# Transposed block inverses in a buffer of their own, and made first

## The chip, the cores and the metric

The kernel runs on one core of one Trainium2 chip. The metric is the device time of one execution in microseconds (us). The engines are TensorE (PE; its weight loads are shown apart as PEld), VectorE (DVE), ScalarE (ACT), GpSimd (POOL) and SyncE (SP), which issues nearly all DMAs. Each engine works through its own instructions in the order in which they stand in the program.

## The reference

One inference step of a two-layer trunk over 128 context and 512 latent tokens (640 in all, width 1024). Each layer runs three mixers side by side: grouped attention (A), latent attention (B), and a recurrent mixer (C) with 8 heads of 64 channels, run over the tokens forwards and backwards. The change lies in mixer C, whose recurrence per head is

```
sa    = einsum('bhij,bhj->bhi', state, a_t)
state = state * w_t + sa ⊗ b_t + v_t ⊗ k_t
y_t   = einsum('bhij,bhj->bhi', state, r_t)
```

The kernel does this in chunks of 64 tokens: inside a chunk the terms `sa` of all tokens solve a unit triangular system, so it needs the inverse of one 64x64 triangular matrix for each head, direction and chunk.

## The kernel before

**Tiling and stages.** Activations lie channel-major, 128 channels to a tile, 640 tokens along the free dimension. A layer has a phase of input projections and mixer C, then attention, then merge and output projection. Mixer C takes the heads in four pairs `p` = 0 to 3; with two layers that makes eight rounds, called here the first to the eighth. A round has these steps:

- `c_inproj` and `c_prep`: projections of key and receptance, decays, the operands `L1` and `BK` (DVE lines 546 to 553);
- `c_pairs`: 40 products on PE into `pA` (line 612), masked into `L1` and `AB` (lines 615, 617, 620 to 625), and transposes of `BK` (lines 632 to 636);
- `c_inverse`: the inverse of the 40 triangular matrices, in place in `AB`; the change lies here;
- `c_scan`: the recurrence over the chunks, with short PE products that wait for ACT and DVE in turn (lines 771 to 803);
- `c_gn` and `c_out` (lines 818 to 852): group normalisation and output.

**The inverse.** A 64x64 matrix is taken as 2x2 blocks of 32x32. Lines 653 and 655 copy the two diagonal blocks of all matrices into `NF`, line 656 transposes them, so that one partition of `LN` holds a whole 32x32 block. Thirty steps of substitution follow on DVE (lines 662 and 664), each needing the one before. Then line 666 transposes the inverses back into `NF`, lines 671 (ACT) and 673 (DVE) copy them into the diagonal of `AB`, and line 674 writes into the same `NF` the inverses once more, this time transposed within each block. PE takes those as moving operand of the first product `px` (line 683, 32x32 matmuls); its result goes to `X1`, which lies in `LN` (lines 688 DVE, 690 ACT), and enters the second product `py` (line 695), whose result becomes the off-diagonal block of `AB` (lines 700, 702). `py` also reads the copies of lines 671 and 673; `px` does not: it reads `NF` and the off-diagonal block of `AB`.

**What sets the order.** The program is written as generators: while the scan of round `p` is written, `pump` writes pieces of the next round's projections, pairs and inverse and of independent projections, called fillers here (the matmuls of lines 227 to 229 and their weight preparation on ACT line 176 and DVE line 177). The table `PLAN` says how many fillers go to each round. The context manager `TileContext(..., schedule_with_timeline_sim=True)` then sets the order of instructions on each engine when the program is built, so a change in one place can move instructions in others. The buffers `NF` and `LN` exist once and serve all rounds.

Of the kernel before, what the change touches and what calls it, by code (L numbers as in the profile page):

```python
# [10 lines left out]
F32 = mybir.dt.float32  # L11
# [82 lines left out]
def f32(ap):  # L94
    return ap.bitcast(F32)
# [12 lines left out]
class Trunk:  # L108
# [230 lines left out]
    def c_open(self, ctx, ctx2, l):  # L339
        tc, nc, I = self.tc, self.nc, self.I  # L340

        def pool(ctx, name, bufs, **k):
            return ctx.enter_context(tc.tile_pool(name=f"{name}{l}", bufs=bufs, reuse_waits="tile", **k))


        self.ct = pool(ctx, "ct", 5)
        self.ce = ce = pool(ctx, "ce", 1)
        cpe = pool(ctx, "cpe", 1)

        self.cs = pool(ctx2, "cs", 1, side="right")  # L350
        self.cp = [cpe, pool(ctx2, "cpo", 1, side="right")]
        self.cmask = ce.tile([128, T], mybir.dt.bfloat16, tag="cmask", name="cmask")
        self.G.memset(self.cmask, 1.0)
        self.G.memset(self.cmask[:, ::64], 0.0)
        self.amask = ce.tile([128, 2, 128], F32, tag="amask", name="amask")
        nc.sync.dma_start(out=self.amask, in_=I["amask"])
        self.NF = ce.tile([128, 1024], F32, tag="NF", name="NF")
        self.LN = ce.tile([128, 1024], F32, tag="LN", name="LN")
        self.G.memset(self.NF, 0.0)

        self.wul = ce.tile([128, 2, 128], F32R, tag="wul", name="wul")
        self.wua = ce.tile([128, 2, 128], F32, tag="wua", name="wua")

        self.wbd = [self.cs.tile([128, 2, 2, 64], F32, tag=f"wbd{i}", name=f"wbd{i}") for i in range(2)]
        self.ubd = [self.cs.tile([128, 2, 2, 64], F32, tag=f"ubd{i}", name=f"ubd{i}") for i in range(2)]
        for t_ in (self.wul, self.wua, *self.wbd, *self.ubd):
            self.G.memset(t_ if t_ is not self.wul else f32(t_), 0.0)
# [270 lines left out]
    def c_inverse(self, e, ps):  # L638

        V, S, G, PE = self.V, self.S, self.G, self.PE  # L640
        AB = e.AB

        def pc(name):
            return ps.tile([128, 512], F32, tag="g", name=name)


        NF, LN = self.NF, self.LN
        NFv = NF.rearrange("p (t u) -> p u t", u=32)
        for q in range(4):
            rows = slice(32 * q, 32 * q + 32)  # L650
            cs_ = slice(32 * (q % 2), 32 * (q % 2) + 32)
            if q % 2:
                S.copy(out=NFv[rows, 0:20, :], in_=AB[rows, :, 0, cs_])
            else:
                V.tensor_copy(out=NFv[rows, 0:20, :], in_=AB[rows, :, 0, cs_])
        V.transpose(out=LN, in_=NF)
        LNv = LN.rearrange("p (a b) -> p a b", b=32)
        prt = NF
        for s in range(1, 31):
            m = 31 - s  # L660
            pv_ = prt[:, 0:m * s].rearrange("p (a b) -> p a b", b=s)
            V.tensor_tensor(out=pv_, in0=LNv[:, s + 1:32, s:s + 1].to_broadcast([128, m, s]),
                            in1=LNv[:, s:s + 1, 0:s].to_broadcast([128, m, s]), op=ALU.mult)
            V.tensor_tensor(out=LNv[:, s + 1:32, 0:s], in0=LNv[:, s + 1:32, 0:s], in1=pv_, op=ALU.add)
        G.memset(LN[:, 0:1024:33], 1.0)
        V.transpose(out=NF, in_=LN)
        for q in range(4):
            rows = slice(32 * q, 32 * q + 32)
            cs_ = slice(32 * (q % 2), 32 * (q % 2) + 32)
            if q % 2 == 0:  # L670
                S.copy(out=AB[rows, :, 0, cs_], in_=NFv[rows, 0:20, :])
            else:
                V.tensor_copy(out=AB[rows, :, 0, cs_], in_=NFv[rows, 0:20, :])
        V.transpose(out=NF, in_=LN.rearrange("p (a b) -> p b a", b=32))

        A0 = (slice(0, 32), slice(64, 96))
        A1 = (slice(32, 64), slice(96, 128))
        X1 = LN[:, 0:T].rearrange("p (u x) -> p u x", x=32)
        for u0, n in ((0, 10), (10, 10)):
            px = pc("px")  # L680
            for h in range(2):
                for j in range(n):
                    PE.matmul(px[A1[h], j * 32:j * 32 + 32], lhsT=AB[A0[h], u0 + j, 0, 32:64],
                              rhs=NFv[A0[h], u0 + j, :], start=True, stop=True)
            for h in range(2):
                src = px[A1[h], 0:n * 32].rearrange("p (u x) -> p u x", x=32)
                if u0 == 0:
                    V.tensor_copy(out=X1[A1[h], u0:u0 + n], in_=src)
                else:
                    S.copy(out=X1[A1[h], u0:u0 + n], in_=src)  # L690
        for u0, n in ((0, 10), (10, 10)):
            py = pc("py")
            for h in range(2):
                for j in range(n):
                    PE.matmul(py[A0[h], j * 32:j * 32 + 32], lhsT=X1[A1[h], u0 + j, :],
                              rhs=AB[A1[h], u0 + j, 0, 32:64], start=True, stop=True)
            for h in range(2):
                src = py[A0[h], 0:n * 32].rearrange("p (u x) -> p u x", x=32)
                if u0 == 0:
                    V.tensor_copy(out=AB[A0[h], u0:u0 + n, 0, 32:64], in_=src)  # L700
                else:
                    S.copy(out=AB[A0[h], u0:u0 + n, 0, 32:64], in_=src)
# [939 lines left out]
```

## Time and profile before

| | us |
|---|---|
| median of 3 runs | 2241.67 |
| lowest and highest | 2239.26 to 2246.77 |
| the profiled execution: its time | 2248.71 |
| its span, first to last instruction | 2246.9 |
| mean granted TensorE clock, share of 2.4 GHz | 0.954 |

The profiled execution is 7.0 us above the median, and 1.8 us of it lie outside the span. The page of the profile gives busy time and share of each engine, the timeline the single instructions with the idle time of the engine just before them in brackets and what ended it; the windows give the granted clock of a stretch.

### The profile page before, as it was taken

Reading aid. Unit: us, or ns where it says so; the run is one execution under the profiler, and the core shown is the slowest. Engines: PE = TensorE matmul, PEld = TensorE weight load, DVE = VectorE, ACT = ScalarE, POOL = GpSimd, SP = SyncE. Lnnn points to the kernel's source line nnn. Section 1 sums busy time; section 2 is a strip of 40 time slices with the busy share of each in tenths; the row PEclk is TensorE's granted clock in tenths of the full one; section 3 lists DMA queues with packets and bytes.
Section 4 is the critical chain, followed back from the end, with each engine's and each line's share of the span. In section 5 each row is a group of like instructions: output and inputs, shape, how many; then the busy total and the mean of one; then the engine's idle time right before and its main releaser. Section 6 shows DMA issues by size and latency. Waiting matters only on the chain.

```text
span 2246.9 us, 40407 instructions
## 1 busy us (share of the span) xinstructions
PE 2095.5 (93%) x15380; PEld 1993.5 (89%) x15380; DVE 1519.9 (68%) x2998; ACT 1200.9 (53%) x2734; POOL 448.1 (20%) x618
## 2 busy tenths in 40 slices
PE   8999999999789889999989999999998888899998
PEld 6989999999779768889989999999997777788998
DVE  4676887857645677766647767668575567776673
ACT  4544656556353667762345455555453546776332
POOL 3111223213121221102030012222221231111112
PEclk9998999999799899999999999899896999999999
DMA  6232222232223211036612222222222221111552
GB/s 235 79 96 73 91 81 98 92 101 86 88 83 127 84 39 40 32 103 207 198 54 86 96 76 90 64 91 90 81 91 67 94 85 42 34 48 60 183 186 84
DMA packets 111762, 209.70 MB, mean 93 GB/s; under 512 B 14416, under 2 KB 33488, under 8 KB 111568
## 3 DMA queue, kind: packets, MB, share of 16 engines
q1 hardware_dynamic: 111568, 207.12, 28.5%
q8 instruction: 121, 1.98, 0.4%
q14 instruction: 73, 0.60, 0.1%
HBM read 163.52 MB, written 43.55 MB: 92 GB/s over the span
## 4 chain that ended last, share of the span: by engine, by line
PE 73%; DVE 11%; ACT 8%; issue 3%; DMA 3%; POOL 1%; SPq 0%; DVEq 0%; ACTq 0%; POOLq 0%
PE pcm L227 11%; PE pcm L228 11%; PE pcm L229 11%; PE pA L612 3%; PE sc L958 3%; PE sca L771 3%; PE pm L180 2%; PE pm L182 2%; PE pm L181 2%; PE pp L976 2%; PE scb L786 2%; PE scb L777 2%; PE sca L790 2%; PE pout L180 1%; PE pout L182 1%
## 5 line engine op out<-in xcount | busy, mean ns | idle before, releaser
L227 PE MATMUL pcm<-hh,whi 128*128 128x320 f32 x1952 | 628.0, 322 | 19.6 <-ACT xlo L380 4.6
L229 PE MATMUL pcm<-hh,wlo 128*128 128x320 f32 x1952 | 618.2, 317 | 3.5 <-DVE wlo L177 3.5
L228 PE MATMUL pcm<-hl,whi 128*128 128x320 f32 x1952 | 618.6, 317 | 0.0
L227 PEld LDWEIGHTS pcm<-hh,whi 128*128 128x128 f32 x1952 | 374.9, 192 | 27.6 <-ACT xlo L380 5.1
L229 PEld LDWEIGHTS pcm<-hh,wlo 128*128 128x128 f32 x1952 | 374.1, 192 | 5.4 <-DVE wlo L177 4.2
L228 PEld LDWEIGHTS pcm<-hl,whi 128*128 128x128 f32 x1952 | 374.8, 192 | 1.3
L176 ACT CAST whi<-wraw 128x512 fp32r<-128x512 f32 (+1 forms) x356 | 226.1, 666 | 274.8 <-PE pcm L228 109.7
L177 DVE TENSOR_TENSOR wlo<-wraw,whi 128x512 fp32r<-128x512 f32 (+1 forms) x324 | 248.6, 785 | 119.1 <-ACT whi L176 113.8
L782 POOL COPY ubd<-VZ 64x128 f32<-64x128 f32 x160 | 63.3, 395 | 457.0 <-ACT VZ L779 450.5
L961 DVE TENSOR_REDUCE nm<-sc 128x1 f32<-128x640 f32 x128 | 104.3, 819 | 26.9 <-PE sc L958 25.5
L166 DVE TENSOR_TENSOR pl<-pp,ph 128x512 fp32r<-128x512 f32 x160 | 107.1, 684 | 22.2 <-ACT ph L165 19.4
L182 PE MATMUL pm<-yh,wlo 128*128 128x320 f32 x384 | 118.9, 310 | 0.3 <-DVE wlo L177 0.3
L180 PE MATMUL pm<-yh,whi 128*128 128x320 f32 x384 | 118.8, 309 | 0.0
L181 PE MATMUL pm<-yl,whi 128*128 128x320 f32 x384 | 118.7, 309 | 0.0
L963 ACT ACTIVATE P<-sc,nm 128x640 f32<-128x640 f32 x128 | 102.1, 799 | 25.7 <-DVE nm L961 20.8
L165 ACT CAST ph<-pp 128x512 fp32r<-128x512 f32 x160 | 91.8, 588 | 37.9 <-PE pp L976 20.4
L976 PE MATMUL pp<-small,P 128*128 128x128 f32 x640 | 98.2, 278 | 2.7 <-ACT RB L1004 2.2
L771 PE MATMUL sca<-VZ,L 128*128 128x64 f32 x640 | 91.5, 284 | 1.7 <-DVE VZ L803 1.7
L771 PEld LDWEIGHTS sca<-VZ,L 128*128 128x128 f32 x640 | 89.1, 207 | 3.1 <-DVE VZ L803 2.8
L803 DVE SCALAR_TENSOR_TENSOR VZ<-scb,gm,Zg 64x64 f32<-64x64 f32 x256 | 62.2, 280 | 40.6 <-PE scb L786 33.6
L976 PEld LDWEIGHTS pp<-small,P 128*128 128x128 f32 x640 | 78.0, 143 | 12.8 <-ACT RB L1004 4.3
L612 PE MATMUL pA<-L,BK 128*128 128x128 f32 x640 | 85.5, 276 | 4.0 <-ACT AB L617 3.7
(376 smaller groups left out, 4748.7 us busy)
## 6 DMA issues: line engine op xcount, KB each, us to landing
wraw<-in_win SPq DMA_DIRECT2D x156, 256.0 KB, 3.0
wraw<-in_wg SPq DMA_DIRECT2D x96, 256.0 KB, 3.0
wraw<-in_wmod SPq DMA_DIRECT2D x64, 256.0 KB, 3.0
gsp<-gt SPq DMA_DIRECT2D x48, 320.0 KB, 3.3
gt<-gsp SPq DMA_DIRECT2D x48, 320.0 KB, 3.4
wraw<-in_wo SPq DMA_DIRECT2D x24, 512.0 KB, 4.2
cm<-gsl SPq DMA_DIRECT2D x26, 320.0 KB, 3.4
wraw<-in_wmod SPq DMA_DIRECT2D x16, 512.0 KB, 6.5
```

The lines of the kernel that those rows point to most:

```text
L166: self.V.tensor_tensor(out=lo, in0=src, in1=f32(hi), op=ALU.subtract)
L176: self.S.copy(out=hi[part], in_=raw)
L177: sub.tensor_tensor(out=lo[part], in0=raw, in1=f32(hi[part]), op=ALU.subtract)
L180: self.PE.matmul(out, lhsT=lh, rhs=rh, start=first, stop=False)
L181: self.PE.matmul(out, lhsT=lh, rhs=rl, start=False, stop=False)
L182: self.PE.matmul(out, lhsT=ll, rhs=rh, start=False, stop=last)
L227: PE.matmul(p[0:m, 0:H], lhsT=wh[:, kt], rhs=self.hh[:, kt, rs], start=(kt == 0), stop=False)
L228: PE.matmul(p[0:m, 0:H], lhsT=wh[:, kt], rhs=self.hl[:, kt, rs], start=False, stop=False)
L229: PE.matmul(p[0:m, 0:H], lhsT=wl[:, kt], rhs=self.hh[:, kt, rs], start=False, stop=(kt == KT - 1))
L612: PE.matmul(pA[:, j * 128:(j + 1) * 128], lhsT=BK[:, u].rearrange("p a s -> p (a s)"), rhs=L1[h][:, u].rearrange("p a s -> p (a s)"), star ...
L771: PE.matmul(a4[:, d, h], lhsT=L1[h][:, uu[d]].rearrange("p a s -> p (a s)"), rhs=VZ[h][:, cc[d], :], start=(h == 0 and d == 0), stop=False ...
L976: PE.transpose(p[:, qt * 128:(qt + 1) * 128], Ps[qt][:, t * 128:(t + 1) * 128], self.ident)
```

## The change

The transposed inverses get a buffer `NT` of their own. Their transposition moves from behind the copies of lines 671 and 673 to the place right behind the substitution, ahead of the plain transposition of line 666; `px` reads `NT` instead of `NF`. The same instructions are executed, as many as before. Lines behind the edit have higher numbers in the changed program: line 666 becomes 671, 671 and 673 become 676 and 678, 674 becomes 670, 683 becomes 687, and from 675 on a line moves by 4; the lines from 359 to 665 move by 1.

```diff
+        self.NT = ce.tile([128, 1024], F32, tag="NT", name="NT")
...
         G.memset(LN[:, 0:1024:33], 1.0)
+
+        NT = self.NT
+        NTv = NT.rearrange("p (t u) -> p u t", u=32)
+        V.transpose(out=NT, in_=LN.rearrange("p (a b) -> p b a", b=32))
         V.transpose(out=NF, in_=LN)
         for q in range(4):
...
                 V.tensor_copy(out=AB[rows, :, 0, cs_], in_=NFv[rows, 0:20, :])
-        V.transpose(out=NF, in_=LN.rearrange("p (a b) -> p b a", b=32))
...
                     PE.matmul(px[A1[h], j * 32:j * 32 + 32], lhsT=AB[A0[h], u0 + j, 0, 32:64],
-                              rhs=NFv[A0[h], u0 + j, :], start=True, stop=True)
+                              rhs=NTv[A0[h], u0 + j, :], start=True, stop=True)
```

The scheduler answers with a new order from the first inverse on: on PE the first 1055 and the last 2348 of 13350 matmuls stand as before, and in between many have moved. Three places matter below, all in the fourth round (layer 0, `p` = 3).

On DVE, the end of the substitution and what follows it, before:

```order
L662 TENSOR_TENSOR NF<-LN 128x30
L664 TENSOR_TENSOR LN<-LN,NF 128x30
L666 STREAM_TRANSPOSE NF<-LN 128x1024
L673 COPY AB<-NF 32x20x32 x2
L674 STREAM_TRANSPOSE NF<-LN 128x1024
L688 COPY LN<-px 32x320 x2
L700 COPY AB<-py 32x10x32 x2
```

On DVE, the same place now (`L` is the operand `L1` of the round before, written by its group normalisation; `wlo` is a filler's weight):

```order
L663 TENSOR_TENSOR NF<-LN 128x30
L665 TENSOR_TENSOR LN<-LN,NF 128x30
L834 TENSOR_TENSOR BK<-BK,gsb 128x640
L177 TENSOR_TENSOR wlo<-wraw,whi 128x512
L670 STREAM_TRANSPOSE NT<-LN 128x1024
L671 STREAM_TRANSPOSE NF<-LN 128x1024
L837 TENSOR_TENSOR L_3528<-BK,lnx 128x10x64
L177 TENSOR_TENSOR wlo<-wraw,whi 128x512
L678 COPY AB<-NF 32x20x32 x2
L692 COPY LN<-px 32x320 x2
L177 TENSOR_TENSOR wlo<-wraw,whi 128x512
L704 COPY AB<-py 32x10x32 x2
```

The transposition that feeds `px` has moved ahead of the other one and of the copies; four instructions of other work have come in around it.

On PE, around the last pair products `pA` of this round, before:

```order
L612 MATMUL pA<-L_4990,BK 128x128 x4
L771 MATMUL sca<-VZ,L_3527 128x64
L771 MATMUL sca<-VZ,L_3528 128x64 x2
L227 MATMUL pcm<-hh,whi 128x320
L228 MATMUL pcm<-hl,whi 128x320
L229 MATMUL pcm<-hh,wlo 128x320
L227 MATMUL pcm<-hh,whi 128x320
L228 MATMUL pcm<-hl,whi 128x320
L229 MATMUL pcm<-hh,wlo 128x320
L227 MATMUL pcm<-hh,whi 128x320
L228 MATMUL pcm<-hl,whi 128x320
L229 MATMUL pcm<-hh,wlo 128x320
```

On PE, the same place now:

```order
L613 MATMUL pA<-L_4991,BK 128x128 x4
L775 MATMUL sca<-VZ,L_3528 128x64 x2
L775 MATMUL sca<-VZ,L_3529 128x64 x2
L227 MATMUL pcm<-hh,whi 128x320
L228 MATMUL pcm<-hl,whi 128x320
L613 MATMUL pA<-L_4991,BK 128x128 x2
L229 MATMUL pcm<-hh,wlo 128x320
```

The last two products of the round stood behind nine fillers and now stand behind two; counted over the whole order, the last one is number 3268 of PE's matmuls instead of 3326, and 214 fillers lie between it and the first `px` instead of 156.

On PE, around `px` of this round, before:

```order
L899 MATMUL pqt<-small,qcm 128x128 x5
L683 MATMUL px<-NF,AB 32x32 x40
L695 MATMUL py<-AB,LN 32x32 x40
L571 MATMUL pbn<-prh,bones 128x320
L572 MATMUL pbn<-prl,bones 128x320
```

On PE, the same place now:

```order
L903 MATMUL pqt<-small,qcm 128x128 x2
L687 MATMUL px<-NT,AB 32x32 x40
L903 MATMUL pqt<-small,qcm 128x128 x3
L699 MATMUL py<-AB,LN 32x32 x40
L572 MATMUL pbn<-prh,bones 128x320
```

Three transposes of attention (line 899 of before) have moved between the two products; the first `px` is number 3572 instead of 3575.

## Rows read from the trace of the kernel before

**Rows 1.** The page, part 1: busy us, share of span, count by engine.
```profile
PE 2095.5 (93%) x15380; PEld 1993.5 (89%) x15380; DVE 1519.9 (68%) x2998; ACT 1200.9 (53%) x2734; POOL 448.1 (20%) x618
```

**Rows 2.** Waits of PE: who <- for what: us in total, times, longest.
```profile
PE px L683 <- DVE NF L674: 14.7, 3, 12.7
```

**Rows 3.** Timeline of DVE, fourth inverse: start, us, line, operation, [idle before <-releaser].
```profile
591.78 1.25 DVE L666 STREAM_TRANSPOSE NF<-LN 128x1024 f32<-128x1024 f32 x1
593.06 1.40 DVE L673 COPY AB<-NF 32x640 f32<-32x640 f32 x2
595.63 1.91 DVE L674 STREAM_TRANSPOSE NF<-LN 128x1024 f32<-128x1024 f32 x1 [1.17 <-ACT AB L671]
599.88 0.99 DVE L688 COPY LN<-px 32x320 f32<-32x320 f32 x2 [2.34 <-PE px L683]
```

**Rows 4.** Timeline of PE, the same inverse.
```profile
597.59 3.93 PE L683 MATMUL px<-NF,AB 32*32 32x32 f32 x77 [12.66 <-DVE NF L674]
601.30 0.26 PE L695 MATMUL py<-AB,LN 32*32 32x32 f32 x1
```

**Rows 5.** Timeline of all engines, its last pair product and its chain’s start.
```profile
547.03 0.60 PE L612 MATMUL pA<-L,BK 128*128 128x128 f32 x4
...
551.58 1.25 DVE L656 STREAM_TRANSPOSE LN<-NF 128x1024 f32<-128x1024 f32 x1 [0.88 <-ACT NF L653]
```

**Rows 6.** Waits of DVE from 533 to 552 us, ahead of that chain.
```profile
DVE L L615 <- PE pA L612: 5.7, 5, 2.9
```

**Rows 7.** Timeline of all engines, its first pair product.
```profile
513.37 0.91 DVE L548 TENSOR_TENSOR BK<-kd,TM 128x640 f32<-128x640 f32 x1
...
516.91 0.49 PE L612 MATMUL pA<-L,BK 128*128 128x128 f32 x3
```

**Rows 8.** Line 674: duration ns min/median/max, first and last start.
```profile
L674 DVE STREAM_TRANSPOSE NF<-LN x8: 1901/2038/2105, 194.3 to 1700.8; 128x1024 f32<-128x1024 f32 x8
```

**Rows 9.** Line 833, the same columns.
```profile
L833 DVE TENSOR_TENSOR L<-BK,lnx x8: 785/822/825, 339.5 to 1804.1; 128x640 f32<-128x640 f32 x8
```

**Rows 10.** The page, part 5, line 177: busy, mean ns, idle before.
```profile
L177 DVE TENSOR_TENSOR wlo<-wraw,whi 128x512 fp32r<-128x512 f32 (+1 forms) x324 | 248.6, 785 | 119.1 <-ACT whi L176 113.8
```

**Rows 11.** Timeline of PE, filler matmuls three apart, at 190 us.
```profile
190.10 0.31 PE L227 MATMUL pcm<-hh,whi 128*128 128x320 f32 x1
...
190.54 0.31 PE L227 MATMUL pcm<-hh,whi 128*128 128x320 f32 x1
```

**Rows 12.** Timeline of PE, filler matmuls three apart, at 1444 us.
```profile
1444.39 0.47 PE L227 MATMUL pcm<-hh,whi 128*128 128x320 f32 x1
...
1445.19 0.47 PE L227 MATMUL pcm<-hh,whi 128*128 128x320 f32 x1
```

**Rows 13.** Timeline of all engines, seventh inverse.
```profile
1563.34 1.24 DVE L666 STREAM_TRANSPOSE NF<-LN 128x1024 f32<-128x1024 f32 x1
...
1570.06 0.33 PE L683 MATMUL px<-NF,AB 32*32 32x32 f32 x3 [1.64 <-DVE NF L674]
```

**Rows 14.** Timeline of all engines, eighth inverse.
```profile
1695.06 1.25 DVE L666 STREAM_TRANSPOSE NF<-LN 128x1024 f32<-128x1024 f32 x1
...
1702.77 0.36 PE L683 MATMUL px<-NF,AB 32*32 32x32 f32 x3 [4.09 <-DVE mean L823]
```

**Rows 15.** Windows at half clock: us, PE busy (count), granted clock, DMA share, GB/s.
```profile
201.70:211.90 10.20, 10.20 (x88) 0.50 0.30 98
321.20:328.00 6.80, 6.80 (x74) 0.50 0.08 22
457.70:464.50 6.80, 6.80 (x49) 0.50 0.22 66
587.40:618.10 30.70, 19.04 (x208) 0.50 0.12 38
1300.80:1304.20 3.40, 3.40 (x15) 0.50 0.61 187
1427.10:1447.60 20.50, 19.81 (x161) 0.50 0.16 50
```

## The prediction

> **What bounds the kernel now.** I read the page first: PE is busy for 93% of the span [rows 1], so the kernel gains where PE stops waiting, and hardly where only DVE or ACT work less. Next the table of waits on PE. The product `px` waits for line 674 three times, 14.7 us in all, 12.7 of them in one wait [rows 2]; no other wait in that table is as long. The timelines then show where: the fourth inverse (12.66 us, [rows 4]), the seventh (1.64 us, [rows 13]) and the eighth (4.09 us, booked apart in [rows 14], where the row names a short instruction behind line 674; the transposition is what `px` reads). The rest of the 14.7 us is 0.4 us at the second. At the first, third, fifth and sixth inverse fillers stand ahead of `px` and PE does not wait. So the most that the change can remove directly is 14.7 + 4.1 = 18.8 us, 0.8% of the span.
>
> **What the edit itself does.** Nothing is added or removed: eight transpositions to `NT` in place of eight to `NF`, 2.04 us each [rows 8], no DMA, no new semaphore path between other engines. What is shortened is the way from the end of the substitution to `px`. In the fourth inverse it ran over line 666 (1.25 us), the copies on DVE (1.40) and on ACT, a wait of 1.17 for these, and line 674 (1.91): from 591.78 to the start of `px` at 597.59, 5.8 us [rows 3, 4]. Now it is one transposition of 2.04 us: 3.8 us less. In the seventh it was 6.7 us, in the eighth 7.7 us [rows 13, 14], so 4.7 and 5.7 us less.
>
> The second product does not gain as much. The copies of `px` into `X1` are queued on DVE behind everything that was moved back. In the fourth inverse that is, after `NT`: the plain transposition 1.25, line 833 with 0.82 [rows 9], a filler's line 177 with 0.79 [rows 10], two copies 1.40, and the copies of `px` themselves 0.99 [rows 3]: 5.25 us. `px` takes 3.7 us until `py` starts behind it [rows 4]. So PE, which now starts `px` 3.8 us sooner, idles up to 1.5 us between the products (some of it covered by three transposes that now stand there), and 2.2 us are left of the 3.8. This is the price of the new order, and it hits where no filler stands between the products: the fourth, seventh and eighth. In the seventh only the transposition, two copies and the copies of `px` are in the way, 3.6 us, as long as `px`: nothing lost.
>
> **What the scheduler does with it.** The order shows the larger effect. In the fourth round the last pair product stands 58 matmuls earlier on PE, with 214 fillers instead of 156 between it and `px`, while `px` itself is at the same place in PE's sequence. A filler takes 0.147 us at full clock (0.44 for three, [rows 11]), so 58 are 8.5 us: the substitution can start that much sooner while PE has work for that much longer. Does it start sooner? Before, the last pair product started at 547.03 and the chain at 551.58 [rows 5], and in the 19 us ahead of it DVE waited 5.7 us for just these products [rows 6], so DVE has the room. If the whole 8.5 us come through, the substitution ends at 591.78 − 8.5 = 583.3, `NT` is ready at 585.3, PE arrives at 597.59 − 12.66 = 584.9 and waits 0.4; `py` starts 5.25 us after `NT`, at 590.6 instead of 601.30: 10.7 us gained. If only the 5.7 us come through, 7.9 us. Against it stands a possible new wait: the first pair product of the round is 9.8 us earlier on PE; before, it started 2.6 us after its last operand from DVE was ready (513.37 + 0.91 to 516.91, [rows 7]), and in DVE's order the operands are about 3 us earlier. 9.8 − 2.6 − 3.0 = 4.2 us is the most it can wait, and none if DVE, which waits for PE in this stretch too, moves up as well. Bounds for the fourth inverse: 2.2 us (the chain starts no sooner) to 10.7; I take 8.5, near the middle of 7.9 and 10.7 less a small new wait.
>
> Eighth: four passes of the group normalisation over 640 columns (lines 818 to 828) now stand ahead of the transposition, 4 × 0.82 = 3.3 us. `NT` is ready at 1695.06 + 3.3 + 2.04 = 1700.4, `px` gains 2.4 of its 4.09 us, and `py`, behind 5.3 us of DVE work instead of 3.7 of `px`, gains 0.8. Bounds 0 to 4.1; I take 1.0. Second: its 0.4 us go, since fillers now stand ahead of `px`. Seventh: here the scheduler works against it. The last pair product is 37 matmuls later on PE (5.3 us) and two more normalisation passes (1.6 us) lie inside the chain, while `px` is at the same place. `NT` is ready between 1563.34 + 1.6 + 2.0 = 1567.0 and 5.3 us later, 1572.3, against a start of 1570.06: between 1.6 gained (PE arrives only at 1568.42) and 2.2 lost; I take 0.3 lost. At the other four, `px` has moved forward by 5 to 44 fillers (0.7 to 6.5 us) and what it reads is ready 3.8 us or more sooner; I cost them at nothing, covered by the fillers still ahead of `px`; without that cover each would cost up to the 2.7 us by which the third outruns its 3.8.
>
> **The clock.** After the 32x32 products the granted clock falls to half (1.2 of 2.4 GHz): six such stretches are shown, 3.4 to 30.7 us long [rows 15]. A filler then takes 0.267 instead of 0.147 us [rows 12], so 45% of such a stretch is lost where PE has work. The two shortest before, 6.8 and 3.4 us at the third and fifth inverse, are those with 22 fillers between `px` and `py`. The first and sixth get that form now: from 10.2 and 20.5 to about 5 each, 20.7 us × 0.45 = 9.3 us gained. The second, which had none between, now gets a scan step and six fillers there, the form of the sixth before with 20.5 us: 13.7 us more, 6.2 lost. Net 3.1 gained; since the stretches come in few, coarse lengths I take 1.4, bounds −6 to +9.
>
> **Sum.** 8.5 + 1.0 + 0.4 − 0.3 + 1.4 = 11.0 us. Against the profiled execution's own time: 2248.7 − 11.0 = 2237.7. That execution is 7.0 us above the median of the three runs; I take the difference as the same in an execution at the median, so 2241.7 − 11.0 = 2230.7, say 2231 us. Its own range, from the ends of the fourth inverse and half the clock's bounds: 2224 to 2236.
>
> **Rivals.**
>
> *The wait moves to DVE.* The substitution is bound by DVE's own queue and starts no sooner in the fourth round; then only the shorter way counts: 2.2 + 0.8 + 0.4 − 2.2 = 1.2 us, with the clock's 1.4 about 2.6: 2239, no change that can be told. For it: in the chain itself DVE hardly idles, and PE's order alone does not speed it. Against it: the 5.7 us that DVE waited for PE just ahead of it [rows 6].
>
> *The clock pays it back: slower.* Five of the eight inverses now have other work between the two products (the first, second, third, fifth and sixth). If all take the long form of the sixth, 20.5 us, instead of the 10.2, 6.8, 6.8, 3.4 and 20.5 of before [rows 15], that is 54.8 us more at half clock, times 0.45: 24.6 us lost, 13.6 slower on the whole, 2255. It decides from 24 us more at half clock on (11.0 / 0.45). For it: the sixth. Against it: the third and fifth, whose form four of the five have. The Trainium skill, "TensorE: Matmul & The Clock Gate", section Terms, puts the penalty at the throttled time times one minus the granted share, half of it; by that the 54.8 us would cost 27.4. The rows at either level give a little less.
>
> *The fourth keeps its clock: faster still.* At the fourth inverse the half-clock stretch begins in the wait, 587.40 to 618.10 [rows 15]. If the wait is what brings it, the part behind the start of `py`, 601.3 to 618.1, comes back too: 16.8 × 0.45 = 7.6 us, 2223. For it: it is the longest of the six, and the only one with a wait. Against it: at the first, PE was busy for all 10.20 us and the clock was at half nevertheless [rows 15]. The Trainium skill, same page, section "HAM oscillation — how this bites in real kernels", ties the fall to gaps in which TensorE waits; by that rule the fourth would keep its clock, and the first should not have lost it, which the row contradicts.
>
> **Chances.** Forecast 0.55, DVE's queue 0.25, clock pays back 0.10, fourth keeps its clock 0.10. About 0.3% (6.7 us) is what a measurement of this kernel can tell from no change, so the line runs at 2235. Of the forecast 0.47 lies beyond it and 0.08 within; of the first rival 0.04 faster, 0.18 within, 0.03 slower, since other reordering of some microseconds comes on top; the second is slower, with 0.02 within; the third faster. Faster 0.61, same 0.28, slower 0.11. The range 2218 to 2246 leaves out the far side of the clock rival and the far end of the gains.
>
> **What would show it.** In the changed profile: the transposition to `NT` starts right behind the last step of line 664's successor; the chain of the fourth round starts 6 to 8.5 us sooner relative to PE's work; the wait before `px` there is below 3 us; one to two us of idle time appear before `py` at the fourth and eighth; line 674's successor nearly leaves the table of waits, but for the seventh. The forecast is wrong if `px` still waits over 5 us at the fourth, if the pair products wait several us there, or if the total at half clock, which the mean granted clock shows, moves by over 20 us.

## The result, and the profile after

| | before | after |
|---|---|---|
| median, us (runs) | 2244.22 (4) | 2228.14 (4) |
| lowest and highest | 2239.26 to 2247.83 | 2225.88 to 2231.14 |
| profiled execution: time, span | 2248.71, 2246.9 | 2231.14, 2229.4 |

The ratio is 0.9931, with an interval of [0.9905, 0.9956]: 16 us faster, against 11 forecast. A second series gave 0.9951 [0.9936, 0.9965] (the experiment `again`).

The page of the changed kernel, part 1, shows PE busy for 4.4 us less than before [rows 1]; the other 13.1 of the 17.5 us of span are idle time of PE.

```profile
PE 2091.1 (94%) x15380; PEld 1986.6 (89%) x15380; DVE 1515.3 (68%) x2998; ACT 1199.0 (54%) x2734; POOL 448.2 (20%) x618
```

The waits of PE in the changed kernel: the wait of `px` for its transposition is 6.0 us in all, where it was 14.7, and 4.1 more under another name [rows 2, 14].

```profile
PE px L687 <- DVE NT L670: 6.0, 3, 4.8
```

**The fourth inverse.** DVE's timeline after:

```profile
584.30 2.07 DVE L670 STREAM_TRANSPOSE NT<-LN 128x1024 f32<-128x1024 f32 x1
586.29 1.21 DVE L671 STREAM_TRANSPOSE NF<-LN 128x1024 f32<-128x1024 f32 x1
...
588.84 1.41 DVE L678 COPY AB<-NF 32x640 f32<-32x640 f32 x2
590.28 1.01 DVE L692 COPY LN<-px 32x320 f32<-32x320 f32 x2
```

PE's timeline of the same place:

```profile
586.15 0.38 PE L903 MATMUL pqt<-small,qcm 128*128 128x128 f32 x2
586.46 4.01 PE L687 MATMUL px<-NT,AB 32*32 32x32 f32 x80
590.40 0.90 PE L903 MATMUL pqt<-small,qcm 128*128 128x128 f32 x3
591.50 0.71 PE L699 MATMUL py<-AB,LN 32*32 32x32 f32 x10 [0.20 <-issue]
```

The transposition to `NT` takes 2.07 us and `px` follows it without a wait; before, 12.66 us [rows 3, 4]. Between `px` and `py` the three moved transposes fill all but 0.20 us. The chain's start, all engines:

```profile
538.66 0.61 PE L613 MATMUL pA<-L,BK 128*128 128x128 f32 x4
...
542.81 1.25 DVE L657 STREAM_TRANSPOSE LN<-NF 128x1024 f32<-128x1024 f32 x1
```

The last pair products start 8.4 us sooner and the chain (the substitution, from this transposition on) 8.8 us sooner than before [rows 5]; 2.5 us of that were gained ahead of the second round's `py`. In the 19 us ahead of the chain DVE has no wait for the pair products, where it had 5.7 us [rows 6].

**The seventh inverse**: its last pair product on PE before, at 1519.76 us,

```profile
1519.76 0.60 PE L612 MATMUL pA<-L,BK 128*128 128x128 f32 x4
```

and after, with the end of its chain, all engines:

```profile
1515.27 0.61 PE L613 MATMUL pA<-L,BK 128*128 128x128 f32 x4
```

```profile
1561.08 1.90 DVE L670 STREAM_TRANSPOSE NT<-LN 128x1024 f32<-128x1024 f32 x1
...
1563.03 3.93 PE L687 MATMUL px<-NT,AB 32*32 32x32 f32 x77 [4.78 <-DVE NT L670]
```

`px` now waits 4.78 us instead of 1.64 [rows 13].

**The eighth inverse**, PE: 0.99 us instead of 4.09 before `px` [rows 14], but a new 1.04 before `py`, which waits for the copies of `px`: the row names those on ACT, and those on DVE, behind the two transpositions, end 0.2 us ahead of them.

```profile
1692.28 4.07 PE L687 MATMUL px<-NT,AB 32*32 32x32 f32 x80 [0.99 <-DVE NT L670]
1697.39 0.81 PE L699 MATMUL py<-AB,LN 32*32 32x32 f32 x12 [1.04 <-ACT LN L694]
```

**The clock**: windows of the changed kernel, columns as in [rows 15].

```profile
194.00:197.40 3.40, 3.40 (x15) 0.52 0.01 1
204.00:210.80 6.80, 6.80 (x32) 0.53 0.43 132
317.00:320.40 3.40, 3.40 (x18) 0.50 0.07 19
324.00:334.20 10.20, 10.20 (x43) 0.51 0.23 72
590.00:607.10 17.10, 15.63 (x137) 0.50 0.24 80
1413.00:1416.40 3.40, 3.40 (x16) 0.55 0.30 101
1430.00:1433.40 3.40, 3.40 (x16) 0.54 0.01 5
1693.00:1713.50 20.50, 18.20 (x199) 0.51 0.27 84
```

The sixth fell from 20.5 us at half clock to 3.4 and 3.4; the first kept its 10.2 (3.4 and 6.8); the second rose from 6.8 to 13.6; the fourth has 17.1 us, though PE came to `px` without a wait. The eighth fell to 20.5 us; before, its stretch was the longest of all, and [rows 15] leave it out:

```profile
1700.20:1741.10 40.90, 33.64 (x271) 0.50 0.14 45
```

**Where the time went.** One execution differs from another by some microseconds in any stretch, so the traces were cut at points where PE does the same thing in all of them: the first product of line 571, right behind a round's `py` and called its read-out below, and the first product of the second layer's key normalisation (line 476). Each cell is the stretch in us and, in brackets, PE's idle time and the time at half clock in it; in the last stretch the idle time counts up to PE's last product.

```
                 start to 2nd      to layer 1        to 5th          to 7th          to the end
inverses in it   1st, 2nd          3rd, 4th          5th             6th, 7th        8th
before           326.4 (19.2,22.3) 868.6 (67.8,73.3) 116.2 (0, 3.4)  266.4 (3.7,27.6) 669.3 (52.9,82.2)
before_twice     326.6 (17.8,25.9) 868.4 (69.1,62.8) 116.2 (0, 3.4)  266.2 (4.1,24.1) 669.6 (52.9,82.5)
after            323.9 (18.4,17.2) 858.3 (54.3,61.3) 117.3 (0, 3.4)  271.1 (10.5,18.0) 658.9 (47.3,68.3)
again            325.7 (20.4,19.5) 863.0 (56.2,69.3) 117.3 (0, 3.4)  271.3 (10.0,21.7) 660.0 (48.4,69.5)
own_second       322.0 (17.9,14.2) 864.2 (56.7,74.5) 117.7 (0, 3.4)  256.0 (0.8, 6.3) 661.0 (47.1,73.9)
own_second_twice 326.9 (17.9,24.2) 864.5 (57.6,71.4) 117.7 (0, 3.4)  256.6 (1.2, 7.0) 659.0 (46.6,65.1)
first0_second1   332.1 (20.4,34.4) 854.6 (54.3,50.9) 117.7 (0, 3.4)  256.8 (1.2, 7.4) 658.9 (47.1,65.0)
second0_first1   328.6 (16.1,30.9) 860.8 (56.1,68.1) 115.7 (0, 0.0)  272.3 (13.2,16.8) 662.8 (49.0,75.7)
fill_fourth      322.7 (17.3,19.0) 861.0 (56.6,66.4) 116.2 (0, 3.4)  264.4 (2.3,21.5) 661.0 (50.3,67.1)
fill_seventh     323.2 (19.3,16.1) 863.5 (56.7,72.6) 117.3 (0, 3.4)  260.6 (1.9,20.5) 665.3 (52.7,65.9)
```

With the mean of the two profiles of each kernel the change is −1.7, −7.9, +1.1, +4.9 and −10.0 us, together −13.6. The five stretches of the two profiles of before agree within 0.3 us; with the same program the first of `own_second` differs by 4.9 us and the second of the changed kernel by 4.7.

### The profile page after: what moved, and what is told of

It reads as the page before. It is cut to its first block, busy times and chain, and to the rows that moved or that the text cites. A ratio compares the mean times of both kernels' runs of the same rounds, so it can differ in the third digit from the quotient of the medians.

```text
span 2229.4 us, 40381 instructions
## 1 busy us (share of the span) xinstructions
PE 2091.1 (94%) x15380; PEld 1986.6 (89%) x15380; DVE 1515.3 (68%) x2998; ACT 1199.0 (54%) x2734; POOL 448.2 (20%) x618
## 5 line engine op out<-in xcount | busy, mean ns | idle before, releaser
L758 POOL TENSOR_TENSOR Zg<-VZ,gm 64x128 f32<-64x128 f32 x112 | 60.0, 536 | 150.7 <-DVE VZ L807 143.5
```

## The experiments

**again.** The changed kernel, no edit.

> The changed kernel once more, for a second profile of it and a closer ratio. Expected 0.990 to 0.996 of the kernel before; in the trace py of the fourth inverse within 1 us of 591.5, no wait above 1 us before px there, a wait of 4 to 5 us before px of the seventh. What differs between its profile and the first by more than 1 us in a stage is noise of a single execution and explains nothing.

2233.62 us (2228.98 to 2238.88, 6 runs), 0.9951 [0.9936, 0.9965]. The waits came again: none at the fourth, 4.76 us at the seventh, 0.99 and 1.04 at the eighth. The absolute time of `py` at the fourth did not, against the expectation: 596.2 instead of 591.5. Of the 4.7 us 1.3 had come up by the third round's read-out and 3.4 between it and `px`, with the same order. Only differences between like places can be compared across executions, which is what the table does.

**own_second.** The buffer alone: the plain transposition stays first. Against the changed kernel:

```diff
-        V.transpose(out=NT, in_=LN.rearrange("p (a b) -> p b a", b=32))
         V.transpose(out=NF, in_=LN)
+        V.transpose(out=NT, in_=LN.rearrange("p (a b) -> p b a", b=32))
```

> The transposed inverses in a buffer of their own, but made second: the plain transposition first, then the transposed one, then the copies. The order has the fourth round's last pair product at number 3268 and 214 fillers behind it, as in the changed kernel, and the seventh's at 9148 with 261 fillers, as in the kernel before. Theory 'the buffer does it, since the transposition no longer has to wait for the copies out of NF, and the scheduler can then draw the pair products forward': ratio 0.988 to 0.995 to the kernel before, px of the fourth without a wait above 2 us, the wait of the seventh below 1 us instead of 4.8, so as fast as the changed kernel or up to 5 us faster. Rival 'the first place does it': each exposed px (fourth, seventh, eighth) comes 1.25 us later, ratio 0.996 to 0.999, 4 us or more slower than the changed kernel.

2222.27 us (2219.58 to 2223.79, 4 runs), 0.9898 [0.9885, 0.9910]: faster than with the transposition to `NT` first, though `px` of the fourth now waits 0.95 us. At the seventh it waits for nothing; on PE, whose filler matmuls run into `px`:

```profile
1552.59 0.31 PE L229 MATMUL pcm<-hh,wlo 128*128 128x320 f32 x1
1552.83 0.28 PE L687 MATMUL px<-NT,AB 32*32 32x32 f32 x2
```

The stretch with the sixth and seventh is 256 us, 15 less than in the changed kernel and 10 less than before. Making the transposition first is thus not what gains; in layer 1 it loses.

**first0_second1 and second0_first1.** The two orders of the transpositions, one in each layer (`l` is the layer's number), and the reverse. Against the changed kernel, the first of the two runs:

```diff
-        V.transpose(out=NT, in_=LN.rearrange("p (a b) -> p b a", b=32))
-        V.transpose(out=NF, in_=LN)
+        two = [(NT, LN.rearrange("p (a b) -> p b a", b=32)), (NF, LN)]
+        for o_, i_ in two if l == 0 else two[::-1]:
+            V.transpose(out=o_, in_=i_)
```

> The changed kernel in layer 0 (transposed inverses first), the plain transposition first in layer 1. The order of layer 0 is that of the changed kernel, that of layer 1 has 261 fillers ahead of px of the seventh instead of 228. Theory 'what parts the changed kernel from own_second is the seventh inverse alone, where the scheduler put the pair products later': no wait at the seventh, ratio as own_second, 0.988 to 0.992, and 7 to 12 us below the changed kernel on the same chip. Rival 'layer 0 gives the difference': ratio 0.994 to 0.996.

> The reverse: plain transposition first in layer 0, transposed inverses first in layer 1; 212 fillers ahead of px of the seventh. Theory 'the seventh inverse alone': a wait of 5 to 8 us before px there, as slow as the changed kernel or slower, ratio 0.994 to 0.998. Rival 'layer 0 gives the difference': as own_second, 0.988 to 0.992.

With `NT` first in layer 0 only: 2220.20 us (2219.42 to 2221.82, 4 runs), 0.9873 [0.9857, 0.9890], which beats both kernels; from `own_second` it can't be told apart. The reverse: 2242.09 us (2231.87 to 2251.03, 12 runs), 0.9971 [0.9953, 0.9989]. The layer-1 half makes the difference in the seventh's stretch: 256.8 against 272.3 us. PE at the seventh in the reverse:

```profile
1569.81 1.56 PE L688 MATMUL px<-NT,AB 32*32 32x32 f32 x28 [6.97 <-DVE NT L672]
```

The number of fillers between the last pair product and `px` there is 261 in `own_second` and 228 in the changed kernel, 212 in the reverse: the edit's cost at the seventh is the scheduler's placing of the pair products.

**fill_fourth.** No edit; one filler group more goes to the fourth round in `PLAN`.

```diff
-    dict(share=[7, 5, 5, 7, 13], fb=[0, 0, 3], ...
+    dict(share=[7, 5, 5, 8, 12], fb=[0, 0, 4], ...
```

> The kernel before, without the edit, with one filler projection moved from the last round of layer 0 into the fourth (share 7 to 8 and 13 to 12, fb 3 to 4): 226 fillers instead of 156 lie between the last pair product and px of the fourth round. Theory 'the 12.7 us wait of the fourth was a shortage of fillers': 70 x 0.147 = 10.3 us of it go, a wait of 2 to 4 us is left, ratio 0.994 to 0.998, since the way to px is as long as before and the waits at the seventh and eighth stay. Rival 'the way from the substitution to px is what costs': the wait keeps 8 us or more, ratio 0.999 to 1.002.

2225.92 us (2221.60 to 2230.43, 6 runs), 0.9912 [0.9897, 0.9927]: faster than the changed kernel in the same series (`again`, 0.9951), and than expected. 226 instead of 156 fillers stand ahead of `px`, and on PE it starts without a wait:

```profile
594.17 0.31 PE L229 MATMUL pcm<-hh,wlo 128*128 128x320 f32 x1
...
594.63 4.03 PE L683 MATMUL px<-NF,AB 32*32 32x32 f32 x80
...
599.42 0.79 PE L695 MATMUL py<-AB,LN 32*32 32x32 f32 x11
```

The stretch with the fourth falls by 7.5 us, as with the change. That the whole is faster than expected lies mostly in the last stretch, −8.4 us, far from the filler that was added and although `px` of the eighth still waits, for 5.0 us; its cause is told below.

**fill_seventh.** The changed kernel, one filler group moved to the seventh round.

```diff
-    dict(share=[8, 6, 7, 7, 9], fb=[0, 0, 1], ...
+    dict(share=[8, 5, 8, 7, 9], fb=[0, 0, 1], ...
```

> The changed kernel with one filler projection of layer 1 moved from the sixth round's share to the seventh's (share 6, 7 to 5, 8): 249 fillers instead of 228 ahead of px of the seventh, and 28 between its px and py; at the sixth none is left between px and py instead of 23. Theory: the seventh's wait of 4.8 us falls to 1 to 2 us and its stretch at half clock from 17 to 7 us or less, while the sixth's grows from 7 to 10 to 20 us; 2 to 6 us faster than the changed kernel, ratio 0.988 to 0.993. Rival 'fillers are only shifted about': within 2 us of the changed kernel, the sixth or the eighth waiting longer for what the seventh gains.

2232.66 us (2231.00 to 2235.29, 5 runs), 0.9946 [0.9934, 0.9958]. The wait at the seventh went and its stretch fell by 10.6 us, of which 24 fillers that left it for the last stretch are some 3.5 (24 × 0.147). The last stretch rose by 5.9: 2.7 us of wait came at the eighth, yet the way from the seventh's read-out to the eighth's is only 1.2 us longer, fillers included; most of the rise lies in attention, which fell back to its order of before and to 5 us more (told below). The time stayed, as the rival had it, but its reason holds only in part. The waits of PE in this kernel:

```profile
PE px L687 <- DVE NT L670: 3.0, 2, 2.7
```

**loose_before and loose_after.** Before and after with the scheduler's timing off, so that the work stays near its place in the program text: of PE's 15380 matmuls 514 stand otherwise in the one than in the other, of POOL's instructions none.

```diff
-    with tile.TileContext(nc, schedule_with_timeline_sim=True) as tc:
+    with tile.TileContext(nc, schedule_with_timeline_sim=False) as tc:
```

> The kernel before with the scheduler's own timeline switched off (schedule_with_timeline_sim=False), so that the order follows the program's text and its buffers more closely. No theory says how much slower it is; it is there as the partner of loose_after. Expected 1.00 to 1.15 of the kernel before, with waits of PE before px in most of the eight rounds.

> The changed kernel, likewise with the scheduler's timeline off; 2 to 22 us of work have moved around the inverses, by the order. Theory 'the shorter way to px counts by itself wherever PE waits for px': 2 to 5 us for each round in which loose_before waits, so 8 to 40 us below loose_before. Rival 'without fillers drawn behind the pair products the edit is worth nothing': within 5 us of loose_before.

2436.78 us (2435.12 to 2438.59, 4 runs) and 2420.75 us (2412.23 to 2424.68, 5 runs); against the kernel before 1.0836 [1.0817, 1.0854] and 1.0760 [1.0736, 1.0784]. So the edit is worth 16 us where the scheduler moves little. `px` waited in nearly every round; page, part 1, and the waits of PE, without the edit:

```profile
PE 2177.4 (89%) x15380; PEld 2019.5 (83%) x15380; DVE 1531.0 (63%) x2998; ACT 1204.0 (49%) x2734; POOL 461.2 (19%) x618
PE px L683 <- DVE NF L674: 24.2, 7, 6.3
```

And with it:

```profile
PE 2171.6 (90%) x15380; PEld 2013.8 (83%) x15380; DVE 1527.8 (63%) x2998; ACT 1204.9 (50%) x2734; POOL 459.7 (19%) x618
PE px L687 <- DVE NT L670: 18.6, 8, 4.1
```

The spans are 15.5 us apart (2434.4 and 2418.9). The waits of `px` are 5.6 us of that, over eight rounds. PE's busy time is another 5.8; it goes with 25.0 us less at half clock (292.9 to 267.9), which would be 11 by the prediction's 45%. The other 4.1 us are idle time of PE elsewhere, and what brought them is not shown. The 16 us are 2.0 a round, less than the 3.8 by which the way to `px` became shorter [rows 3, 4].

**after_fill4 and own2_fill4.** The filler group of `fill_fourth` on top of the changed kernel and of `own_second` (the same diff).

> The changed kernel together with that filler; 234 fillers ahead of px of the fourth, but 212 instead of 228 of the seventh. Theory: the fourth has no wait to lose any more; the seventh waits 2 to 3 us longer (16 x 0.147) than the 4.8 of the changed kernel; so between equal and 5 us slower than it, ratio 0.993 to 0.998, and slower than fill_fourth, which lacks the edit. Rival 'separate gains': 0.983 to 0.988.

> own_second (own buffer, plain transposition first) together with the filler that fill_fourth moved into the fourth round; 240 fillers ahead of px of the fourth, 252 of the seventh. Theory 'both removed one and the same wait at the fourth': within 4 us of own_second, ratio 0.986 to 0.991, no wait above 0.5 us at the fourth or seventh. Rival 'the two are separate gains': about 15 us below own_second, ratio 0.980 to 0.984.

2232.51 us (2230.65 to 2234.70, 6 runs), 0.9938 [0.9924, 0.9952]: no gain beside the change, and 6.97 us of wait at the seventh instead of 4.78, as the theory had it. On `own_second` 2233.45 us (2222.40 to 2239.02, 6 runs), 0.9941 [0.9920, 0.9963]: 11 us slower than without the filler, which neither theory nor rival had. Its seventh, on PE, waits twice:

```profile
1564.18 4.07 PE L687 MATMUL px<-NT,AB 32*32 32x32 f32 x80 [1.94 <-DVE NT L671]
1569.57 0.44 PE L699 MATMUL py<-AB,LN 32*32 32x32 f32 x5 [1.31 <-ACT LN L694]
```

The stretch with it is 268.7 us against 256. There the seventh's first pair product stands behind 237 fillers instead of 205, counted from the sixth's read-out, and starts 57.3 us behind it instead of 47.1; in the changed kernel it is 245 and 58.2. So the scheduler has put the pair products later there too; why this filler moves it to do so stays open.

**before_twice and own_second_twice.** The two kernels unchanged, a second profile each, to tell chance of one execution from order.

> The kernel before, unchanged: a second profile, for what one execution differs from another by stretch. The stretches run between the same PE places (the first product with `bones` of a round). If the eighth inverse's gain in the changed kernel is its order, the stretch from there to the end is again 669 us here, with some 41 us at half clock behind the eighth inverse; if it is chance of one execution, about 661 us, with 20 to 24 us at half clock. The other stretches: 868.6 us from the third to the fifth round within 5, with 12 to 13 us of wait before `px` at the fourth; 266.4 us around the sixth and seventh inverse within 3. Time 2240 to 2249.

> The own buffer with the plain transposition first, unchanged, a second profile. If the order at the seventh inverse decides against the changed kernel (271 us in two profiles), the stretch around the sixth and seventh is again 256 us within 2, with no wait before `px`; if that was chance, 262 to 271. The stretch to the end, 661.0 in the first profile with 41 us at half clock: 658 to 664 by either. Time 2219 to 2225.

2249.08 and 2226.41 us, one run each, 0.1 and 1.4 us above what was expected. The last stretch of before came again at 669.6 us with 41.0 us at half clock, 10 us over both profiles of the changed kernel. `own_second` again had 256.6 us around the seventh, so the order decides there; but at its eighth the time at half clock was 20.5 us instead of 41.0, with the same order. So the part of the 10 us that goes with the half clock may be chance of the execution.

## What the last stretch gained

The 10.0 us of the last stretch are mainly three things, which sum to 10.7; 0.7 is lost again elsewhere. From the seventh's read-out to the eighth's: 2.0 us, the eighth inverse itself (132.6 to 130.6). Then matmuls 51 to 100 behind it: 14.6 us in both profiles of before, 11.0 and 11.1 in those of the changed kernel, which goes with the length of the half clock: `own_second`, with 41.0 us of it in one profile and 20.5 in the other, had 14.6 and 10.5. So 20.5 us at half clock cost 3.5 to 4.1 here, not 45%. Then, in attention of the second layer, matmuls 701 to 900: 42.0 us in both profiles of before, 36.8 in both of the changed kernel. The timeline of before there, all engines:

```profile
1848.39 4.65 DVE L871 TENSOR_TENSOR rp<-q,ropeA 128x64 f32<-128x64 f32 x8
...
1849.94 2.49 POOL L177 TENSOR_TENSOR wlo<-wraw,whi 128x512 fp32r<-128x512 f32 x2
...
1852.97 0.81 DVE L961 TENSOR_REDUCE nm<-sc 128x1 f32<-128x640 f32 x1
...
1854.75 0.64 PE L958 MATMUL sc<-KT,QT 128*128 128x320 f32 x1 [4.47 <-ACT P L963]
```

And of the changed kernel:

```profile
1833.49 1.75 DVE L875 TENSOR_TENSOR rp<-q,ropeA 128x64 f32<-128x64 f32 x8
...
1835.42 2.98 POOL L177 TENSOR_TENSOR wlo<-wraw,whi 128x512 fp32r<-128x512 f32 x2 [1.07 <-ACT whi L176]
...
1835.95 1.55 DVE L965 TENSOR_REDUCE nm<-sc 128x1 f32<-128x640 f32 x2
...
1837.74 0.56 PE L962 MATMUL sc<-KT,QT 128*128 128x320 f32 x2 [1.24 <-ACT P L967]
```

Eight products of 128x64 take 4.65 us on DVE before and 1.75 after. POOL's two products of line 177 run beside them before and start behind them after. The softmax's maximum (line 961, now 965) queues behind the eight, and PE waits 4.47 us for its exponentials, now 1.24. This goes with the order of PE's matmuls 641 to 752 of the stretch, not with the edit: `fill_seventh`, which has the edit and the old order there, takes 42.0 us for these 200; `fill_fourth`, without the edit and with the new order, 36.8.

## Why the prediction was right, and where only its sum was

- **Forecast**: 2231 in a range of 2218 to 2246; 2228.14 was measured, and 2233.62 in the second series. Two of its terms were off by 5 and 9 us in opposite directions, so the sum is better than its parts: that it came so near is in part luck.
- **Fourth inverse, 8.5 us**: its steps were right. Chain 8.8 us sooner (8.5 taken), and 10.3 sooner counted from PE's arrival at `px` (43.7 us ahead of it instead of 33.4), `px` without a wait (0.4), no new wait ahead of the pair products (up to 4.2 feared), 0.20 and 0.56 us between the products (up to 1.5). The stretch up to layer 1 fell by 7.9 us. 41 fillers went from the third round into the fourth, so the two must be taken together: from the second's read-out to the fourth's 4.8 us were gained (278.8 and 276.3 to 271.4 and 274.2), the rest behind it. PE was idle for 11.3 us less in the two rounds, but busy for 6.6 us longer with the same matmuls; 7.7 us more at half clock with PE at work are an estimated 3.5 of these (45%), and the rest is not accounted for. `fill_fourth` takes the same wait away without the edit and gains the same in this stretch; both together gain no more. What both gave PE at the fourth is the cover that it lacked.
- **Seventh, 0.3 lost**: mis-sized, and its bound of 2.2 too. From the last pair product to the end of `NT` the chain takes 47.8 us (1515.27 to the start of `px`, 1563.03), 2.5 less than before (1519.76 to 1570.06); but PE has work for only 43.0 us of it (to 1558.26), where it had 48.7. The difference is the 4.8 us. The value taken lay amid bounds, though the row was clear on one half: 37 matmuls less cover are 5.3 us. The new order also brought waits of 0.84, 1.30 and 1.49 us into that round (0.83, 1.12 and 1.34 in the second profile), which no step looked for.
- **Eighth, 1.0**: its own part measured 2.0. Not foreseen were the other 8 us, behind it: the half clock and attention. The prediction did not look at the wait of 4.47 us in attention, since nothing was edited there; the scheduler moved it all the same.
- **Clock, 1.4**: right in form for the sixth (20.5 to 6.8) and the second (6.8 to 13.6 and 17.1), not for the eighth (41.0 to 20.5, no term). The first, for which 10.2 to 5 was taken, came to 10.2 and 3.4. In all, 208.8 and 198.7 us at half clock (the rows of the table added up) became 168.2 and 183.4, 28 less; by the prediction's own sign, over 20 us, the clock step was wrong in size. So was its price: 45% of 28 us would be 12.6, yet PE's busy time fell by only 2.7 (2095.5 twice, to 2091.1 and 2094.5). The 45% were read from fillers in close order [rows 11, 12]; in the scan behind the eighth inverse PE has gaps (33.64 busy of 40.90 us), and there half clock cost less.
- **Rivals.** *The wait moves to DVE*: fell, the chain started 8.8 us sooner. *The clock pays it back*: fell, five interleaved rounds have 3.4 to 17.1 us each. *The fourth keeps its clock*: fell too; no wait, yet 17.1 us at half clock behind the 32x32 products. The Trainium skill, "TensorE: Matmul & The Clock Gate", section "HAM oscillation — how this bites in real kernels", ties the fall to gaps; here the trace disagrees, at the fourth as at the first.

Still open: what ends the stretch at half clock behind the eighth inverse after 20.5 or 41.0 us with the same order, and why the filler on `own_second` moves the seventh's pair products.

## What to carry to other kernels

A buffer written twice ties the scheduler as well as the engines: freeing it moved work in places that the edit does not touch, and there lay much of the gain and nearly all of the loss. Where an in-order engine waits, count the work that stands ahead of the waiting instruction against the length of the chain it waits for; a filler can do what an edit does, and the two don't add. Test the parts of an edit apart: the buffer gained, and the order of the two transpositions, which came with it, lost in one layer and told nothing in the other.

## What the runs showed of the hardware

A DVE product of 128x64 with two operands takes 0.21 us alone and up to 1.30 us beside a POOL product of 128x512: the eight of line 871 above took 1.00, 0.74, 1.30, 1.29 and four times 0.21 us, and the 1.30 and 1.29 are, within 0.04, the lengths of the POOL products beside them (1.27 and 1.26, 2.49 for the two). The Trainium skill, "SBUF — State Buffer", section "SBUF: two separate sides", says that DVE and GpSimd share a pair of ports that one of them holds for a whole instruction; the rows agree.

The clock falls after 32x32 products in which PE was busy throughout (at the first inverse of before 10.20 of 10.20 us at half clock [rows 15], with no wait ahead of them), and how long it stays down differs between executions of one program. Behind the eighth inverse of `own_second`, first and second profile:

```profile
1680.00:1721.00 41.00, 35.12 (x275) 0.50 0.16 53
```

```profile
1688.50:1709.00 20.50, 17.96 (x176) 0.50 0.27 84
```
